# The RWKV-7 recurrence in two chains of four units instead of four chains of two, with its operands kept in DRAM records

## The chip, the cores and the metric

The kernel runs on one core of one Trainium2 chip. A core has engines that each work through a program of their own in order: TensorE (PE, matmuls; PEld are its weight loads), VectorE (DVE), ScalarE (ACT), GpSimd (POOL, which here only issues DMAs) and SyncE (SP, which issues the weight loads). They meet through semaphores. The metric is the device time of one execution in microseconds (us); lower is better.

## What is computed

One decoder layer on x of 256 tokens by 4096 columns, all in float32. Cut to what matters:

```python
h = rms_norm(x, norm_pre_g)
proj = einsum('btd,dc->btc', h, w_in)          # 4096 -> 14528 columns
rwkv_in, g_rwkv, glu_v, glu_g, g_conv = split(proj, ...)
xs = rwkv_in + (shift(rwkv_in) - rwkv_in) * mu_shift
r, k, v, w_low, a_low = split(xs, ...)
# 32 heads of 64; per step t and head, with a state S of 64 x 64:
S = S * w_t + (S @ -kk_t) b_t^T + v_t k_t^T ;  y_t = S @ r_t
y_rwkv = (group_norm(y) + bonus) * silu(g_rwkv)
c = silu(layer_norm(causal_conv31(glu_v * sigmoid(glu_g)))) @ w_pw2 + b_pw2
y_conv = c * silu(g_conv)
out = concat(y_rwkv, y_conv) @ w_out
return x + rms_norm(out, norm_post_g)
```

The recurrence is done in chunks of 32 tokens (8 chunks), with matrices inside a chunk and the state S handed from chunk to chunk.

## The kernel before

**The main stream.** The three projections (w_in, w_pw2, w_out) are 41 blocks of mostly 512 columns. A block runs through k-tiles of 128 rows, and one k-tile of a block is a slot: 1248 slots, each with six matmuls of 512 columns (two halves of the tokens, each with hi by hi, hi by lo and lo by hi, since a float32 product is made of fp32r parts). For each slot SP loads weights (`wr`, 512 KB for two slots, four buffers), ACT rounds them (`wh`), DVE takes the rest (`wl`), each with five buffers, three to four slots ahead of PE.

**The side work.** All that stands between the projections (the token shift, the preparation of the recurrence, its chain, the conv, the norms, the gates) is written as generators in lanes. After each slot's six matmuls `side.step()` lets the lanes go on; a generator that says `yield` gives up the rest of this slot, so that what follows it stands at least one slot later. The meters (`Meter`) add up an estimated cost on DVE and ACT and stop the lanes of a slot when these are ahead of PE. PE, DVE and ACT run in the order in which the code is written down; POOL and SP are ordered by a scheduler. Almost every instruction goes through the meter's line 92, so tiles and not lines tell them apart.

**The recurrence.** The 32 heads are 8 units of 4 heads. `job_prep(u)` makes a unit's operands: `c_ar` (decayed r and kk), `c_q` (masked products inside chunks, by PE), `c_bkt` (decayed b and k, turned by PE) and `c_uv` (v, turned). `job_inv(pr)` inverts the triangular parts of two units on DVE, by way of the DRAM tiles `n_dr` and `x_dr`, into `c_x`. `job_chain(pr)` takes a pair of units through the 8 chunks together. Per chunk PE has three visits to the PSUM tile `pz`, between them ACT and DVE:

- RY: `c_q` by `c_uv`, and from the second chunk on `c_ar` by the state `c_s`; then ACT copies the sum to `c_ry`;
- RU: `c_x` by `c_ry`; then ACT and DVE, half the rows each, write it negated into `c_uv`;
- RD and RO: `c_bkt` by `c_uv` (the state's change, not in the last chunk) and `c_q` by `c_uv` (the outputs); then DVE makes the outputs `c_y` and the next `c_s`.

Each of these products is 8 matmuls in the program for a pair (2 units by 4 quadrants of the array); the trace shows two records for each, so 16. A chain is 24 visits, the four pairs make 96. After a chain come a group norm over `c_y` and the store of the unit's result to `y_dr`. The conv's layer norm and the gates (`job_ln`, `job_gate`) wait in `open_conv` for the last chain, since they take over the SBUF of the recurrence; the w_pw2 blocks, from slot 928 on, need the layer norm's `chl`.

Of the kernel before, what the change touches and what calls it, by code (L numbers as in the profile page):

```python
# [9 lines left out]
F32 = mybir.dt.float32  # L10
F32R = mybir.dt.float32r
AF = mybir.ActivationFunctionType
# [5 lines left out]
P = 128  # L18
# [159 lines left out]
def hybrid(ctx: ExitStack, tc, a, out):  # L178
# [18 lines left out]
    sgc_dr = dr.tile([4, P, 1024], F32, name="sgc_dr")  # L197
    n_dr = dr.tile([8, 4, 8, CH, CH], F32, name="n_dr")
# [54 lines left out]
    def tp_put():  # L253

        tpf[0] += 1
# [29 lines left out]
    def x_load(i):  # L285
        if i % 2 == 0:
            st["xc"] = rw["pool"].tile([P, 8, T + 1], F32, name=XTAG[i // 2], bufs=1)
        t = st["xc"][:, 4 * (i % 2):4 * (i % 2) + 4, :]
# [138 lines left out]
    def job_prep(u):  # L427
# [71 lines left out]
        pr, un = u // 2, u % 2  # L499
        if un == 0:  # L500
            while pr and not rw.get(("chained", pr - 1)):
                yield "wait"
            rw["pair", pr] = dict(ar=rp.tile([P, 2, 16, 64], F32, name="c_ar", bufs=1),
                                  qs=rp.tile([P, 2, 2, NCH, 64], F32, name="c_q", bufs=1),
                                  bkt=rp.tile([P, 2, NCH, 2, 64], F32, name="c_bkt", bufs=1),
                                  uv=rp.tile([P, 2, NCH, 2, 64], F32, name="c_uv", bufs=1),
                                  pc=one.tile([P, 2, 16], F32, name="c_pc"))
        pair = rw["pair", pr]
        ar, qs, bkt, uv, pc = (pair[k][:, un] for k in ("ar", "qs", "bkt", "uv", "pc"))
# [46 lines left out]
        rw[("n", u)] = True  # L556

        bp = yield from head_sums(bq, "t_sw")
        if un == 0:
            while pr and not rw.get(("done", pr - 1)):  # L560
                yield "wait"
            pair["bv"] = rp.tile([P, 2, 512], F32, name="c_bv", bufs=1)
        vec.tensor_tensor(out=pair["bv"][:, un], in0=bp, in1=vs[:, 0:512], op=ALU.mult)
# [11 lines left out]
        for h in range(2):  # L575
            for e in range(2):
                act(out=uv[:, e::2, h], in_=t[h], func=AF.Copy)
            tp_put()
        rw[("prepd", u)] = True
        yield  # L580

    def job_inv(pr):

        rp = rw["pool"]
        while ("n", 2 * pr + 1) not in rw or (pr and not rw.get(("done", pr - 1))):
            yield "wait"
# [24 lines left out]
        xt = rp.tile([P, 2, 8, CH], F32, name="c_x", bufs=1)  # L611
# [7 lines left out]
        rw["pair", pr]["xt"] = xt  # L619

    def job_chain(pr):

        rp = rw["pool"]
        while ("prepd", 2 * pr + 1) not in rw or "xt" not in rw["pair", pr]:
            yield "wait"
        d = rw.pop(("pair", pr))
        ar, qs, bkt, uv, pc, bv, xt = (d[k] for k in ("ar", "qs", "bkt", "uv", "pc", "bv", "xt"))
        ys = rp.tile([P, 4, 2, 2, 64], F32, name="c_y", bufs=1)
        S = pz = ry = None
        RY, RU, RO, RD = (slice(i * 64, i * 64 + 64) for i in range(4))  # L630
        UN = range(2)
# [4 lines left out]
        def outputs(c):  # L636
            for rows in (slice(0, P),) if c % 2 == 0 else KS:
                vec.tensor_tensor(out=ys[rows, c // 2], in0=swap(pz[rows, :, :, RO]), in1=ry[rows], op=ALU.add)

        for c in range(NCH):  # L640
            vr, ur = VR[c % 2], UR[c % 2]
            if c > 0:
                outputs(c - 1)
                Sn = rp.tile([P, 2, 2, 64], F32, name="c_s", bufs=2)
                dec = pc[:, :, c - 1::8].unsqueeze(3).broadcast_to([P, 2, 2, 64])
                if S is None:
                    vec.tensor_tensor(out=Sn, in0=swap(pz[:, :, :, RD]), in1=dec, op=ALU.mult)
                else:
                    vec.tensor_tensor(out=Sn, in0=swap(pz[:, :, :, RD]), in1=S, op=ALU.add)
                    vec.tensor_tensor(out=Sn, in0=Sn, in1=dec, op=ALU.mult)  # L650
                S = Sn
                yield
            pz = ps_ch.tile([P, 2, 2, 256], F32, name="pz")

            for n in UN:
                for q, h in DIAG:
                    pe.matmul(pz[HS[q], h, n, RY], qs[vr[q ^ h], n, h, c, :], uv[vr[q ^ h], n, c, h, :], start=n == 0, stop=S is None and n == 1)
            for n in UN if S is not None else ():
                for q, h in DIAG:
                    pe.matmul(pz[HS[q], h, n, RY], ar[HS[h], n, q * 8 + c, :], S[HS[h], n, q, :], start=False, stop=n == 1)  # L660
            yield
            ry = rp.tile([P, 2, 2, 64], F32, name="c_ry", bufs=1)
            act(out=ry, in_=swap(pz[:, :, :, RY]), func=AF.Copy)
            for n in UN:
                for q, h in DIAG:
                    pe.matmul(pz[ur[q ^ h], h, n, RU], xt[ur[q], n, h * 4 + c // 2, :], ry[ur[q], n, h, :], start=True, stop=True)
            yield
            act(out=uv[ur[0], :, c], in_=swap(pz[ur[0], :, :, RU]), func=AF.Copy, scale=-1.0)
            vec.tensor_scalar(out=uv[ur[1], :, c], in0=swap(pz[ur[1], :, :, RU]), scalar1=-1.0, scalar2=None, op0=ALU.mult)
            for n in UN if c < NCH - 1 else ():  # L670
                for q, h in DIAG:
                    pe.matmul(pz[HS[h], q, n, RD], bkt[HS[q ^ h], n, c, h, :], uv[HS[q ^ h], n, c, h, :], start=True, stop=True)
            for n in UN:
                for q, h in DIAG:

                    ro, k0 = (KS, CH) if c % 2 else (HS, 0)
                    pe.matmul(pz[ro[q], h, n, RO], qs[ur[q ^ h], n, h, c, k0:], uv[ur[q ^ h], n, c, h, :], start=True, stop=True)
            yield
        outputs(NCH - 1)
        rw[("chained", pr)] = True  # L680
        yield 0

        mv = rp.tile([P, 2, 16], F32, name="c_mv", bufs=1)
        mn, vr = mv[:, 0], mv[:, 1]
        y3 = ys.rearrange("p c n h x -> p (c n h) x")
        for b in range(2):
# [4 lines left out]
        for b in range(2):  # L691
# [15 lines left out]
        for b in range(2):  # L707
# [5 lines left out]
        for n in UN:  # L713
            u = 2 * pr + n
            yo = rp.tile([P, 16, CH], F32, name="c_sq", bufs=1)
            bv3 = bv[:, n].rearrange("p (c t) -> p c t", t=CH)
# [12 lines left out]
            if n == 0:  # L729
                for _ in range(6):  # L730
                    yield
        rw[("done", pr)] = True
# [156 lines left out]
    def ev_shift(kind, g):  # L889
        def f(acc):  # L890
# [6 lines left out]
            if kind == "v":  # L897
# [3 lines left out]
                side.add("2", job_chain(g))  # L901
# [31 lines left out]
    def open_conv():  # L933
        while not rw.get(("done", 3)):
            yield "wait"
# [322 lines left out]
```

## Time and profile before

| | |
|---|---|
| median of 3 runs | 1850.20 us (1850.18 to 1852.35) |
| the profiled execution's own time | 1850.36 us |
| its span, first to last instruction | 1848.5 us |
| PE busy | 1835.3 us (99%) |
| DVE busy | 1345.9 us (73%) |
| ACT busy | 1024.4 us (55%) |
| POOL busy | 118.3 us (6%), 218 instructions |
| DMA | 367.19 MB, mean 199 GB/s |

PE's clock is granted in full (0.998 in the mean, that is 2.4 GHz). A busy PE here counts each matmul to its modelled end, which lies after the start of the next one; what a stretch of PE really costs is read from the starts in the timeline.

### The profile page before, as it was taken

What the parts mean: (1) busy time and instruction counts of PE and PEld (TensorE: products, weight loads), DVE (VectorE), ACT (ScalarE), POOL (GpSimd) and SP (SyncE); (2) the same over time, 40 slices, a digit from 0 to 9 for tenths busy, and PEclk for the clock granted to TensorE, in tenths of its full rate; (3) what the DMA queues carried; (4) which work ended last, traced back from release to release, by engine and by line L of the source; (5) the groups of instructions that cost most, each with busy time, mean ns of one, the idle gap of its engine ahead of it and who ended that gap; (6) DMA issues with size and microseconds to landing.
All of it is one profiled execution on the core that took longest, in us unless ns stands there. A gap on an engine that the chain in (4) does not pass through costs nothing.

```text
span 1848.5 us, 31244 instructions
## 1 busy us (share of the span) xinstructions
PE 1835.3 (99%) x11569; PEld 1495.3 (81%) x11569; DVE 1345.9 (73%) x2630; ACT 1024.4 (55%) x1785; POOL 118.3 (6%) x218
## 2 busy tenths in 40 slices
PE   9999999999999999999999999999999999999997
PEld 7899888877888877888778888788888888888886
DVE  6655679987689988799877899667656655555555
ACT  6756665546655555655465655356645444445453
POOL 0000001300000300011200003010000000000000
PEclk9999999999999999999999999999999999999999
DMA  9867667755667746676546677468776766666665
GB/s 329 271 177 203 177 180 198 215 148 146 191 189 204 205 124 180 179 206 197 163 143 200 175 223 217 147 208 277 214 233 204 246 194 199 199 200 194 204 198 190
DMA packets 193863, 367.19 MB, mean 199 GB/s; under 512 B 14384, under 2 KB 31920, under 8 KB 193456
## 3 DMA queue, kind: packets, MB, share of 16 engines
q1 hardware_dynamic: 182352, 335.31, 60.7%
q0 software_dynamic: 11360, 29.90, 5.3%
q8 instruction: 90, 1.47, 0.3%
q14 instruction: 61, 0.50, 0.1%
HBM read 352.57 MB, written 12.58 MB: 198 GB/s over the span
## 4 chain that ended last, share of the span: by engine, by line
PE 98%; DVE 1%; DMA 0%; ACT 0%; SPq 0%; issue 0%; DVEq 0%
PE acc L92 92%; PE tp L92 4%; PE pz L92 3%; DMA wr<-in_w_in 0%; DVE chl L92 0%; DVE wl L92 0%; DVE t_pi L92 0%; ACT L92 0%; SPq L291 0%; ACT wh L92 0%; DVE c_y L92 0%; SPq L1104 0%; ACT tp L92 0%; DVEq L1236 0%; ACT t_sw L92 0%
## 5 line engine op out<-in xcount | busy, mean ns | idle before, releaser
L92 ACT ACTIVATE wh<-wr 128x512 fp32r<-128x512 f32 (+1 forms) x1243 | 770.4, 624 | 655.2 <-PE acc L92 372.4
L92 DVE TENSOR_TENSOR wl<-wr,wh 128x512 fp32r<-128x512 f32 (+1 forms) x1243 | 831.5, 677 | 339.9 <-ACT wh L92 335.4
L92 PE MATMUL acc<-wh,lh 128*128 128x512 f32 (+1 forms) x2358 | 927.9, 394 | 1.0 <-ACT wh L92 0.9
L92 PE MATMUL acc<-wl,lh 128*128 128x512 f32 (+1 forms) x2358 | 911.0, 386 | 0.5 <-DVE wl L92 0.5
L92 PE MATMUL acc<-wh,ll 128*128 128x512 f32 (+1 forms) x2358 | 911.1, 386 | 0.0
L92 PEld LDWEIGHTS acc<-wh,lh 128*128 128x128 f32 x2358 | 442.8, 188 | 92.5 <-ACT wh L92 2.1
L92 PEld LDWEIGHTS acc<-wh,ll 128*128 128x128 f32 x2358 | 442.8, 188 | 89.3
L92 PEld LDWEIGHTS acc<-wl,lh 128*128 128x128 f32 x2358 | 443.2, 188 | 83.5 <-DVE wl L92 1.5
L92 DVE SCALAR_TENSOR_TENSOR cw<-up,pv,cw 128x256 f32<-128x256 f32 x480 | 216.6, 477 | 0.4
L92 PE MATMUL acc<-wh,chl 128*128 128x512 f32 x256 | 82.5, 397 | 0.0
L92 PEld LDWEIGHTS acc<-wh,chl 128*128 128x128 f32 x256 | 48.1, 188 | 11.1
L92 DVE TENSOR_SCALAR c_uv<-pz 32x256 f32<-32x256 f32 x32 | 13.6, 426 | 51.7 <-ACT c_uv L92 51.7
L92 PE MATMUL acc<-wl,chl 128*128 128x512 f32 x128 | 50.5, 395 | 0.0
L554 POOL DMA_DIRECT2D n_dr<-c_q x32 | 18.6, 589 | 489.0 <-DVE c_q L92 438.3
L92 ACT ACT_TABLE_LOAD x38 | 48.8, 1283 | 1.8 <-PEq L1230 0.7
L615 POOL DMA_DIRECT2D c_x<-x_dr x64 | 34.8, 551 | 14.0 <-DMA x_dr<-t_x 11.0
L92 ACT ACTIVATE c_ry<-pz 128x256 f32<-128x256 f32 x32 | 12.3, 384 | 41.0 <-PE pz L92 31.5
L92 ACT ACTIVATE pt<-acc,rstd 128x512 f32<-128x512 f32 (+3 forms) x52 | 34.0, 657 | 1.7 <-PE acc L92 1.0
L92 DVE TENSOR_TENSOR c_sq<-t_x,c_y 128x120 f32<-128x120 f32 (+24 forms) x124 | 31.8, 257 | 4.0 <-DMA c_y<-n_dr 3.9
L92 DVE TENSOR_TENSOR t_x<-t_x,c_sq 128x120 f32<-128x120 f32 (+24 forms) x124 | 31.7, 256 | 0.1
L92 PEld LDWEIGHTS pz<-c_uv,c_q 32*64 32x64 f32 (+1 forms) x1024 | 19.7, 124 | 14.3 <-issue 12.0
L92 DVE RECIPROCAL t<-t 128x128 f32<-128x128 f32 x32 | 29.8, 940 | 0.3
(172 smaller groups left out, 876.3 us busy)
## 6 DMA issues: line engine op xcount, KB each, us to landing
wr<-in_w_in SPq DMA_DIRECT2D x431, 512.0 KB, 4.2
wr<-in_w_out SPq DMA_DIRECT2D x128, 512.0 KB, 4.4
wr<-in_w_pw SPq DMA_DIRECT2D x32, 512.0 KB, 4.4
wr<-in_w_in SPq DMA_DIRECT2D x16, 352.0 KB, 3.3
c_y<-n_dr POOLq DMA_DIRECT2D x16, 256.0 KB, 6.3
out<-chl SPq DMA_DIRECT2D x16, 256.0 KB, 2.2
wr<-in_w_in SPq DMA_DIRECT2D x16, 192.0 KB, 2.7
wr<-in_w_in SPq DMA_DIRECT2D x16, 160.0 KB, 2.5
```

Of the source, the lines that this page charges most:

```text
L92: return f(*args, **kw)
L554: nc.gpsimd.dma_start(out=n_dr[u, y].rearrange("(h g) k j -> k h g j", h=2), in_=qs[y * CH:(y + 1) * CH, :, 1 - x::2, x * CH:(x + 1) * CH])
L615: nc.gpsimd.dma_start(out=xt[y * CH:(y + 1) * CH, un, h * 4:h * 4 + 4], in_=x_dr[2 * pr + un, y ^ (2 * h), h * 4:h * 4 + 4].rearrange("g i ...
```

## The change

The chains become two, each of four units (a quad) in lockstep, so every product of a visit has 16 matmuls in the program instead of 8. The operands no longer stay in SBUF from preparation to chain: `job_prep` writes `c_ar`, `c_q`, `c_bkt` and `c_uv` of its unit to the DRAM tile `rec_dr` (and the bonus to `bv_dr`), and the chain fetches a record of 1 MB per chunk into `c_st` (two buffers), one chunk ahead. The three tiles RY, RU and RO now lie in the same columns of `pz` (RX). A chunk has more `yield`s between its steps. The inversion of the second pair no longer waits for the first chain. The chain is started only by every second group of columns, and `open_conv` waits for the second quad. The x tiles of the start lie in other buffers.

```diff
@@ job_prep
-        pr, un = u // 2, u % 2
+        qd, un = u // 4, u % 4
         if un == 0:
-            while pr and not rw.get(("chained", pr - 1)):
-                yield "wait"
-            rw["pair", pr] = dict(ar=rp.tile([P, 2, 16, 64], F32, name="c_ar", bufs=1),
...
+            rw["quad", qd] = dict(pc=rp.tile([P, 4, 16], F32, name="c_pc", bufs=2))
+        pc = rw["quad", qd]["pc"][:, un]
+        ar = rp.tile([P, 16, 64], F32, name="c_ar", bufs=1)
+        qs = rp.tile([P, 2, NCH, 64], F32, name="c_q", bufs=1)
...
+        for h in range(2):
+            nc.gpsimd.dma_start(out=rec_dr[qd, :, :, un, 0, h * 64:h * 64 + 64].rearrange("c p x -> p c x"), in_=ar[:, h * 8:h * 8 + 8, :])
+            nc.gpsimd.dma_start(out=rec_dr[qd, :, :, un, 1, h * 64:h * 64 + 64].rearrange("c p x -> p c x"), in_=qs[:, h])
...
+        nc.gpsimd.dma_start(out=bv_dr[u], in_=bv)
...
+        for i, t in ((2, bkt), (3, uv)):
+            nc.gpsimd.dma_start(out=rec_dr[qd, :, :, un, i].rearrange("c p x -> p c x"), in_=t.rearrange("p c h x -> p c (h x)"))
@@ job_inv
-        while ("n", 2 * pr + 1) not in rw or (pr and not rw.get(("done", pr - 1))):
+        while ("n", 2 * pr + 1) not in rw or (pr > 1 and not rw.get(("done", pr // 2 - 1))):
@@ job_chain
+        UN = range(4)
+        def fetch(c):
+            if c < NCH:
+                recs[c] = rp.tile([P, 4, 4, 2, 64], F32, name="c_st", bufs=2)
+                nc.gpsimd.dma_start(out=recs[c].rearrange("p n i h x -> p (n i h x)"), in_=rec_dr[qd, c].rearrange("p n i x -> p (n i x)"))
...
+        fetch(0)
+        for _ in range(8):
+            yield
         for c in range(NCH):
+            fetch(c + 1)
+            ar, qs, bkt, uv = (recs[c][:, :, i] for i in range(4))
             if c > 0:
                 outputs(c - 1)
...
                 yield
+                yield
-            pz = ps_ch.tile([P, 2, 2, 256], F32, name="pz")
+            pz = ps_ch.tile([P, 2, 4, P], F32, name="pz")
...
             yield
-            ry = rp.tile([P, 2, 2, 64], F32, name="c_ry", bufs=1)
-            act(out=ry, in_=swap(pz[:, :, :, RY]), func=AF.Copy)
+            ry = rp.tile([P, 4, 2, 64], F32, name="t_x", bufs=1)
+            act(out=ry, in_=swap(pz[:, :, :, RX]), func=AF.Copy)
+            yield
...
-            act(out=uv[ur[0], :, c], in_=swap(pz[ur[0], :, :, RU]), func=AF.Copy, scale=-1.0)
-            vec.tensor_scalar(out=uv[ur[1], :, c], in0=swap(pz[ur[1], :, :, RU]), scalar1=-1.0, scalar2=None, op0=ALU.mult)
+            act(out=uv[ur[0]], in_=swap(pz[ur[0], :, :, RX]), func=AF.Copy, scale=-1.0)
+            vec.tensor_scalar(out=uv[ur[1]], in0=swap(pz[ur[1], :, :, RX]), scalar1=-1.0, scalar2=None, op0=ALU.mult)
+            yield
...
+            bv = rp.tile([P, 512], F32, name="t_x", bufs=1)
+            nc.gpsimd.dma_start(out=bv, in_=bv_dr[u])
+            for _ in range(6):
+                yield
@@ ev_shift, open_conv
-                side.add("2", job_chain(g))
+                if g % 2:
+                    side.add("2", job_chain(g // 2))
-        while not rw.get(("done", 3)):
+        while not rw.get(("done", 1)):
```

**PE at the start of a chain.** The order of PE's matmuls from the first RU visit to the RD and RO visit of chunk 0, in the first chain; `acc` rows are the main stream, six to a slot. Before:

```order
L92 MATMUL pz<-c_ry,c_x 32x64 x8
L92 MATMUL acc<-wh,lh 128x512
L92 MATMUL acc<-wl,lh 128x512
L92 MATMUL acc<-wh,ll 128x512
L92 MATMUL acc<-wh,lh 128x512
L92 MATMUL acc<-wl,lh 128x512
L92 MATMUL acc<-wh,ll 128x512
L92 MATMUL pz<-c_uv,c_bkt 64x64 x8
L92 MATMUL pz<-c_uv,c_q 64x64 x8
```

With the change the same two visits stand two slots apart, twelve main matmuls instead of six (left out here), and the second is one row of 32, since RD and RO read the same tile `c_st`:

```order
L92 MATMUL acc<-wh,lh 128x512
L92 MATMUL acc<-wl,lh 128x512
L92 MATMUL acc<-wh,ll 128x512
L92 MATMUL pz<-t_x,c_x 32x64 x16
L92 MATMUL acc<-wh,lh 128x512
L92 MATMUL acc<-wl,lh 128x512
L92 MATMUL acc<-wh,ll 128x512
```

What moved: each visit carries twice the matmuls, and it stands one slot further from the visit that it depends on. Over the whole program `pz` is visited 48 times instead of 96, with the same 1216 matmuls in all; the six matmuls of every slot stay as they were.

**POOL around the first chain.** The queue of DMA issues with the change, from the last inversion before the chain (`x_dr`, `c_x`) on; in the kernel before, the load of the next inversion's `t_x` and the conv's `c_dr` follow right behind `c_x` there:

```order
L647 DMA c_st<-rec_dr 128x2048 x2
L794 DMA c_dr<-cw 128x512
L615 DMA x_dr<-t_x 256x1x32 x8
L623 DMA c_x<-x_dr 32x4x32 x16
L647 DMA c_st<-rec_dr 128x2048
L794 DMA c_dr<-cw 128x512
L647 DMA c_st<-rec_dr 128x2048 x4
L560 DMA rec_dr<-c_ar 128x8x64 x2
L647 DMA c_st<-rec_dr 128x2048
L561 DMA rec_dr<-c_q 128x8x64
```

What moved: the eight fetches of a quad stand in the same queue as the record writes of the next unit and the conv's stores, and the first two go out before the inverse is stored. POOL has 282 rows in all instead of 202.

**DVE before the w_pw2 blocks.** The end of the layer norm on DVE, before; `wl` rows are the main stream's, one per slot, and the last `chl` row here stands behind 886 of them:

```order
L92 TENSOR_TENSOR chl<-c_c,chl 128x1024
L92 TENSOR_TENSOR wl<-wr,wh 128x512
L92 SCALAR_TENSOR_TENSOR c_m<-ln_q,pv,tp 128x256 x2
L92 TENSOR_TENSOR c_c<-c_c,ln_r 128x1024
L92 TENSOR_TENSOR wl<-wr,wh 128x512 x9
L92 TENSOR_TENSOR chl<-c_c,chl 128x1024
L92 TENSOR_TENSOR wl<-wr,wh 128x512 x21
```

With the change the last `chl` row stands behind 937 of them:

```order
L92 TENSOR_TENSOR chl<-c_c,chl 128x1024
L92 TENSOR_TENSOR wl<-wr,wh 128x512
L92 TENSOR_TENSOR c_c<-c_c,ln_r 128x1024
L92 TENSOR_TENSOR wl<-wr,wh 128x512 x8
L92 TENSOR_TENSOR chl<-c_c,chl 128x1024
L92 TENSOR_TENSOR wl<-wr,wh 128x512 x2
L92 SCALAR_TENSOR_TENSOR c_m<-ln_q,pv,tp 128x256 x2
```

What moved: the layer norm ends 51 slots later. PE reads its last quarter from slot 940 on.

## Rows read from the trace of the kernel before

**Rows 1.** The page: engines' busy time, and the chain that ended last.

```profile
PE 1835.3 (99%) x11569; PEld 1495.3 (81%) x11569; DVE 1345.9 (73%) x2630; ACT 1024.4 (55%) x1785; POOL 118.3 (6%) x218
...
PE acc L92 92%; PE tp L92 4%; PE pz L92 3%; DMA wr<-in_w_in 0%; DVE chl L92 0%; DVE wl L92 0%; DVE t_pi L92 0%; ACT L92 0%; SPq L291 0%; ACT wh L92 0%; DVE c_y L92 0%; SPq L1104 0%; ACT tp L92 0%; DVEq L1236 0%; ACT t_sw L92 0%
```

**Rows 2.** Waits of ACT: who for whom, us, times, longest us.

```profile
ACT wh L92 <- PE acc L92: 372.4, 532, 3.5
ACT wh L92 <- DMA wr<-in_w_in: 13.6, 9, 2.4
```

**Rows 3.** PE's timeline, RU to RO visit of chunk 0: start, us, what.

```profile
380.42 0.39 PE L92 MATMUL acc<-wh,ll 128*128 128x512 f32 x1
380.74 0.42 PE L92 MATMUL pz<-c_ry,c_x 32*32 32x64 f32 x16
...
381.43 0.39 PE L92 MATMUL acc<-wl,lh 128*128 128x512 f32 x1
381.66 0.39 PE L92 MATMUL acc<-wh,ll 128*128 128x512 f32 x1
...
382.36 0.40 PE L92 MATMUL acc<-wh,ll 128*128 128x512 f32 x1
382.68 0.46 PE L92 MATMUL pz<-c_uv,c_bkt 64*64 64x64 f32 x16
383.07 0.46 PE L92 MATMUL pz<-c_uv,c_q 32*64 32x64 f32 x16
...
383.80 0.40 PE L92 MATMUL acc<-wl,lh 128*128 128x512 f32 x1
```

**Rows 4.** PE's timeline, the first RY visit, which has one product only.

```profile
378.44 0.39 PE L92 MATMUL acc<-wh,ll 128*128 128x512 f32 x1
378.76 0.46 PE L92 MATMUL pz<-c_uv,c_q 32*64 32x64 f32 x16
...
379.49 0.40 PE L92 MATMUL acc<-wl,lh 128*128 128x512 f32 x1
```

**Rows 5.** PE's timeline, two longer visits of the same small shape, in the preparation.

```profile
217.42 0.39 PE L92 MATMUL acc<-wh,ll 128*128 128x512 f32 x1
217.74 1.16 PE L92 MATMUL tp<-c_ar,t_bk 64*64 64x64 f32 x64
...
219.17 0.39 PE L92 MATMUL acc<-wl,lh 128*128 128x512 f32 x1
...
231.39 0.39 PE L92 MATMUL acc<-wh,ll 128*128 128x512 f32 x1
231.71 0.69 PE L92 MATMUL tp<-cst,t_bk 64*64 64x64 f32 x32
...
232.67 0.39 PE L92 MATMUL acc<-wl,lh 128*128 128x512 f32 x1
```

**Rows 6.** The timeline of ACT and DVE between the visits of rows 3.

```profile
381.23 0.37 ACT L92 ACTIVATE c_uv<-pz 32x256 f32<-32x256 f32 x1 [1.03 <-PE pz L92]
...
381.64 0.43 DVE L92 TENSOR_SCALAR c_uv<-pz 32x256 f32<-32x256 f32 x1 [2.15 <-ACT c_uv L92]
```

**Rows 7.** Instructions of 512 columns by tile: ns min/median/max, first and last start.

```profile
L92 DVE TENSOR_TENSOR c_y<-c_y,c_mv x16: 680/688/693, 449.4 to 1225.3; 128x512 f32<-128x512 f32 x16
...
L92 ACT ACTIVATE c_sq<-c_y x8: 615/618/633, 450.2 to 1218.8; 128x512 f32<-128x512 f32 x8
```

**Rows 8.** DMA: POOL's queue (packets, MB, share), and one issue (KB, us to landing).

```profile
q0 software_dynamic: 11360, 29.90, 5.3%
...
c_c<-in_x POOLq DMA_DIRECT2D x1, 2048.0 KB, 11.1
```

**Rows 9.** Busy time and DMA of 1225 to 1300 us, where the layer norm's loads run.

```profile
1225.00:1300.00 75.00, 75.00 (x340) 62.04 (x339) 53.33 (x78) 45.12 (x70) 7.43 (x14) 1.00 0.81 260
```

**Rows 10.** Waits of ACT in that same stretch.

```profile
ACT wh L92 <- DMA wr<-in_w_in: 8.8, 5, 2.3
```

More of the change, by code (lines that the diff above doesn't have):

```diff
@@ L556, in job_prep @@
         rw[("n", u)] = True
+        for h in range(2):
+            nc.gpsimd.dma_start(out=rec_dr[qd, :, :, un, 0, h * 64:h * 64 + 64].rearrange("c p x -> p c x"), in_=ar[:, h * 8:h * 8 + 8, :])
+            nc.gpsimd.dma_start(out=rec_dr[qd, :, :, un, 1, h * 64:h * 64 + 64].rearrange("c p x -> p c x"), in_=qs[:, h])
         bp = yield from head_sums(bq, "t_sw")
[L559 to L563, printed above, removed]
+        bv = rp.tile([P, 512], F32, name="c_bv", bufs=1)
+        vec.tensor_tensor(out=bv, in0=bp, in1=vs[:, 0:512], op=ALU.mult)
+        nc.gpsimd.dma_start(out=bv_dr[u], in_=bv)
         tp_put()
@@ L610, in job_inv @@
                 nc.gpsimd.dma_start(out=xv[rho][:, un], in_=xi[rho * 32:(rho + 1) * 32, un])
-        xt = rp.tile([P, 2, 8, CH], F32, name="c_x", bufs=1)
+        quad = rw["quad", pr // 2]
+        if pr % 2 == 0:
+            quad["x"] = rp.tile([P, 4, 8, CH], F32, name="c_x", bufs=1)
+        xt = quad["x"][:, pr % 2 * 2:pr % 2 * 2 + 2]
         for y in range(4):
@@ L618, in job_inv, with job_chain @@
             yield
-        rw["pair", pr]["xt"] = xt
-    def job_chain(pr):
+        if pr % 2:
+            quad["xt"] = quad["x"]
+    def job_chain(qd):
         rp = rw["pool"]
-        while ("prepd", 2 * pr + 1) not in rw or "xt" not in rw["pair", pr]:
+        while ("prepd", 4 * qd + 3) not in rw or "xt" not in rw["quad", qd]:
             yield "wait"
-        d = rw.pop(("pair", pr))
-        ar, qs, bkt, uv, pc, bv, xt = (d[k] for k in ("ar", "qs", "bkt", "uv", "pc", "bv", "xt"))
-        ys = rp.tile([P, 4, 2, 2, 64], F32, name="c_y", bufs=1)
+        d = rw.pop(("quad", qd))
+        pc, xt = d["pc"], d["xt"]
+        ys = rp.tile([P, 4, 4, 2, 64], F32, name="c_y", bufs=1)
         S = pz = ry = None
-        RY, RU, RO, RD = (slice(i * 64, i * 64 + 64) for i in range(4))
-        UN = range(2)
+        RX, RD = slice(0, 64), slice(64, 128)
+        UN = range(4)
+        recs = {}
+        def fetch(c):
+            if c < NCH:
+                recs[c] = rp.tile([P, 4, 4, 2, 64], F32, name="c_st", bufs=2)
+                nc.gpsimd.dma_start(out=recs[c].rearrange("p n i h x -> p (n i h x)"), in_=rec_dr[qd, c].rearrange("p n i x -> p (n i x)"))
         def swap(x):
@@ L676, in job_chain @@
                     ro, k0 = (KS, CH) if c % 2 else (HS, 0)
-                    pe.matmul(pz[ro[q], h, n, RO], qs[ur[q ^ h], n, h, c, k0:], uv[ur[q ^ h], n, c, h, :], start=True, stop=True)
+                    pe.matmul(pz[ro[q], h, n, RX], qs[ur[q ^ h], n, h, k0:], uv[ur[q ^ h], n, h, :], start=True, stop=True)
             yield
         outputs(NCH - 1)
-        rw[("chained", pr)] = True
         yield 0
-        mv = rp.tile([P, 2, 16], F32, name="c_mv", bufs=1)
+        mv = rp.tile([P, 2, 32], F32, name="c_mv", bufs=1)
         mn, vr = mv[:, 0], mv[:, 1]
         y3 = ys.rearrange("p c n h x -> p (c n h) x")
-        for b in range(2):
+        for b in range(4):
             sl = slice(b * 8, b * 8 + 8)
@@ L690, in job_chain @@
         vec.tensor_scalar(out=mn, in0=mn, scalar1=1.0 / 64, scalar2=None, op0=ALU.mult)
-        for b in range(2):
+        for b in range(4):
             sl = slice(b * 8, b * 8 + 8)
@@ L706, in job_chain @@
         vec.reciprocal(out=vr, in_=vr)
-        for b in range(2):
+        for b in range(4):
             sl = slice(b * 8, b * 8 + 8)
@@ L728, in job_chain @@
             nc.gpsimd.dma_start(out=y_dr[u], in_=yo.rearrange("p c t -> p (c t)"))
[L729 to L732, printed above, removed]
+        rw[("done", qd)] = True
         yield
```

37 lines of the change are left out of this document (19 added, 18 removed).

## The prediction

> **What bounds the kernel now.** I read four views, in this order. First the page's busy times and the chain that ended last: PE is busy 99% of the span, and 92% of the chain is main matmuls (`acc`), 4% transposes and 3% the recurrence's `pz` [rows 1]. So an edit is worth what it takes from PE's own stream of instructions, and nothing else counts unless it becomes later than PE. Second the waits: ACT stood 372.4 us idle until PE gave it a buffer back, but only 13.6 us, in 9 pieces, for weights to land [rows 2]. Both feeders run ahead and are held back by PE, so there is room on ACT and DVE and in the weight stream. Third PE's timeline around the visits to `pz`, for what a visit costs. Busy time can't tell that, since it overlaps; I take starts. Two main matmuls that follow each other start 0.23 us apart (381.43 to 381.66, [rows 3]). A visit's cost is the time from the start of the last main matmul ahead of it to the start of the second one behind it, less two such gaps (0.46 us), because the first matmul behind a visit is slow too. Fourth the DMA rows, for what the records add.
>
> **What the change removes: half of the visits.** A visit with two products of 16 records (RD and RO, or RY with the state) costs 383.80 - 382.36 - 0.46 = 0.98 us. A visit with one product of `c_x` costs 381.43 - 380.42 - 0.46 = 0.55 us [rows 3]. A visit with one product of `c_q` costs 379.49 - 378.44 - 0.46 = 0.59 us [rows 4]. A pair's chain has 14 visits of the first kind (7 RY and 7 RD with RO), 8 RU, and 2 with one product (the first RY, the last RO): 14 x 0.98 + 8 x 0.55 + 2 x 0.59 = 19.3 us. Four pairs: 77.2 us.
>
> **What stays: the matmuls, in longer groups.** Their number is the same, so the question is what a product of 32 records costs beside one of 16. The trace of before has no such `pz` visit, but it has longer visits of the same 64x64 shape over the same four quadrants: 64 records cost 219.17 - 217.42 - 0.46 = 1.29 us, and 32 cost 232.67 - 231.39 - 0.46 = 0.82 us [rows 5]. Thirty-two more records cost 0.47 us, so sixteen more cost 0.235 us. The rest of a visit is paid once per product, however long. That gives 0.98 + 2 x 0.235 = 1.45 us for a double visit, 0.55 + 0.235 = 0.785 for RU and 0.59 + 0.235 = 0.825 for a single one. A quad's chain: 14 x 1.45 + 8 x 0.785 + 2 x 0.825 = 28.2 us; two quads 56.5 us. **The gain on PE is 77.2 - 56.5 = 20.7 us.** The other end of this cost: from the start of the first product to that of the second in a double visit are 383.07 - 382.68 = 0.39 us [rows 3]; if sixteen more records cost all of that again, visits come to 1.76, 0.94 and 0.98 us, a quad to 14 x 1.76 + 8 x 0.94 + 2 x 0.98 = 34.1 us, and the gain is 77.2 - 68.2 = 9.0 us. Below that, at no gain, a product would have to cost twice as much when doubled, and rows 5 exclude it. More than 20.7 us would need the added records to be nearly free, which rows 5 exclude as well. I take 20.7 us, by the nearer rows: same shape, same quadrants, same length as the new groups.
>
> The Trainium skill has a rule that speaks for the lower end: "TensorE: Matmul & The Clock Gate", in the section "Wait — 56ns, not 53.3ns?", says that matmuls never start closer together than about 25 ns, however small they are. By it sixteen more records would cost some 0.40 us. The trace bears it out only in the look of one product (0.39 us for 16); the 64 records that take 1.16 us in all [rows 5], 18 ns each, speak against it, and they count for more.
>
> **What it adds between the visits.** DVE and ACT do the same steps on twice the columns in half as many instructions, so they are relieved. What matters is whether a step is ready when PE comes to the next visit. The tightest hand-over now is RU to RO: the visit starts at 380.74, ACT copies from 381.23 for 0.37 us, DVE from 381.64 for 0.43 us [rows 6], that is to 382.07, and PE comes at 382.68 [rows 3], 0.61 us later. At 512 columns ACT takes 0.62 and DVE 0.69 us [rows 7], 0.51 us more together; the longer RU visit moves both sides by the same 0.235 us, and from its end to RO stand two slots instead of one, 6 x 0.23 = 1.38 us more. The slack grows to 0.61 - 0.51 + 1.38 = 1.5 us. From RO to the next RY DVE has at most four steps of 0.69 us (two outputs, two for the state), 2.8 us, in three or four slots, 4.1 to 5.5 us. So the wider steps cost PE nothing; the cover is the slack just worked out.
>
> **What it adds in DMA.** Per unit 6 record writes and a bonus, 8 x 7 = 56 issues; 16 fetches and 8 loads of the bonus: 80 more on POOL, 0.54 us of POOL each by 118.3 us for 218 instructions [rows 1], 43 us on an engine that is 6% busy. The bytes are 16 MB of records written, 16 read and 4 of bonus. POOL's queue has 29.90 MB at 5.3% of the DMA engines' time [rows 8], so 37.7 (in the page's MB) add about 6.7%. A fetch is one more wait for PE: RY needs the record. The fetch of chunk c+1 can go once RO of chunk c-1 has released the buffer, and RY of c+1 stands 11 slots behind that in the order: 11 x 1.38 us and three visits (1.45 + 0.785 + 1.45), 18.9 us. A load of twice its size landed in 11.1 us [rows 8]. Queued ahead of a fetch on POOL are at most the conv's store and the next unit's record writes, which wait for values that DVE has made some slots earlier. That cover is large, so I cost the fetch at nothing.
>
> **What it moves.** The second quad's chain ends later, and with it the layer norm, by 51 slots. Its last quarter stands behind 937 `wl` rows and is needed at slot 940. DVE is held to PE's pace by five `wl` buffers, so it comes to that row when PE is near slot 933: about 7 x 1.38 = 9.7 us early, where it was some 58 slots early before. No visit and no wait of PE is added there. From slot 943 on the program is the same as before.
>
> **Sum.** The profiled execution took 1850.36 us (span 1848.5 and 1.9 us around it), 0.16 us from the median of 1850.20. 1850.2 - 20.7 = **1829.5 us**, 1.1% less.
>
> **The rivals.**
>
> *Longer groups cost more than rows 5 say.* Gain 9.0 us, **1841.2 us**. For it: `pz` products change their operands per unit and were seen only at 16 records, 0.39 us each. Against it: 64 records in rows 5. The rule on the 25 ns, named above, would end here too, at 0.40 us for each sixteen and about 1841.5 us.
>
> *The layer norm comes late.* Its loads of 2 MB now run with the gates close behind, in 60 slots less room; in the stretch of its loads ACT waited 8.8 us for weights, up to 2.3 us at a time [rows 10], while DMA was at 0.81 and PE lost nothing [rows 9]. If that, and a chain of DVE and ACT steps that slips, outruns the 9.7 us by as much as those 8.8 us, PE waits 8.8 us: **1838.3 us**.
>
> *The hand-overs give it back: no change.* It takes 20.7 / 48 = 0.43 us of waiting per visit. The slack of 1.5 us at the tightest place speaks against it; for it speaks that DVE's queue has conv and preparation between the steps, and is full where the fifth unit is prepared beside the first chain. **About 1850 us.**
>
> *Slower: the fetches starve the weights.* Sixteen fetches of 1 MB come in bursts beside a stream whose weights are needed every two slots. The place is `wh` on ACT in the chain. The largest burst of before, in rows 9 and 10, cost ACT up to 2.3 us at a time, and PE rode over it on the four slots that ACT is ahead, about 5.5 us. If every fetch cost PE those 2.3 us in full, 16 x 2.3 = 36.8 us, the time is 1829.5 + 36.8 = **1866.3 us**. It decides from 20.7 / 16 = 1.3 us per fetch on. Against it: the stock of slots and the 13.6 us in the whole kernel [rows 2]. The Trainium skill, "DMA: Bandwidth & Descriptors", section "Queues, rings and completion order", states the mechanism: an engine takes turns between its queues by packets, so that a second queue takes its share from the weights at once. No row here shows one packet waiting for another; what it would do is what rows 10 show.
>
> *That the change doesn't do what it says* is excluded by the order: 48 visits, and 16 matmuls in each product.
>
> **How the numbers follow.** Forecast 0.67 (own range 1825 to 1834: rounding of starts by 0.01 us over 96 visits, and the 2 us by which the runs differ), longer groups 0.11, late layer norm 0.07, no change 0.07, slower 0.08. A difference of 0.2%, 3.7 us, is about what a measurement of this kernel can tell from none. Faster: 0.67 + 0.11 + 0.07 = 0.85; same 0.07; slower 0.08. The range takes in the first three, 1825 to 1844.
>
> **What would show it.** In the profile of the changed kernel a double visit should take 1.45 us by starts, RU 0.785, with no idle of PE ahead of `pz`; POOL's queue about 68 MB and 12%; PE's idle no more than before; ACT's waits for weights a few tens of us at most. A visit of 1.76 us would show the first rival, PE idle ahead of `acc` with `chl` as the releaser the second, ahead of `pz` the third, and PE idle for `wh` inside the two chains the last. I am wrong at the root if PE's starts show the visits halved and the time the same, for then PE was not what set the pace.

## The result and the profile after

The changed kernel takes 1829.6 us (median of four runs, 1828.7 to 1830.2) beside 1851.1 us of the kernel before on the same chip: a ratio of 0.988, 95% interval 0.987 to 0.990, faster by 21.5 us. The profiled execution took 1830.16 us, 20.2 us less than that of before.

The page of the changed kernel, with the lines that answer to [rows 1] and [rows 8]; columns are the same:

```profile
span 1828.1 us, 31382 instructions
...
PE 1814.0 (99%) x11569; PEld 1492.9 (82%) x11569; DVE 1330.3 (73%) x2560; ACT 1009.2 (55%) x1745; POOL 179.4 (10%) x298
...
q0 software_dynamic: 19808, 67.65, 11.7%
...
PE 93%; DMA 2%; DVE 2%; issue 2%; POOL 1%; ACT 0%; SPq 0%; DVEq 0%; POOLq 0%; ACTq 0%
```

PE has the same 11569 instructions, is busy 21.3 us less and still fills 99% of the span. POOL's queue moves 67.65 MB. In the chain that ended last PE's share has fallen from 98 to 93%; DMA, DVE and time without a visible cause ("issue") have 2% each, POOL 1%. Where they stand is shown below.

Three visits to `pz`, in PE's timeline of the changed kernel (start, us, what): the first RY, RY with the state, and RU. They answer to [rows 3, 4].

```profile
620.26 0.39 PE L92 MATMUL acc<-wh,ll 128*128 128x512 f32 x1
620.58 0.69 PE L92 MATMUL pz<-c_st 32*64 32x64 f32 x32
...
621.54 0.40 PE L92 MATMUL acc<-wl,lh 128*128 128x512 f32 x1
...
1127.91 0.39 PE L92 MATMUL acc<-wh,ll 128*128 128x512 f32 x1
1128.23 0.69 PE L92 MATMUL pz<-c_st 32*64 32x64 f32 x32
1128.85 0.69 PE L92 MATMUL pz<-c_s,c_st 64*64 64x64 f32 x32
1129.48 0.50 PE L92 MATMUL acc<-wh,lh 128*128 128x512 f32 x1
1129.81 0.39 PE L92 MATMUL acc<-wl,lh 128*128 128x512 f32 x1
...
1132.10 0.39 PE L92 MATMUL acc<-wh,ll 128*128 128x512 f32 x1
1132.42 0.65 PE L92 MATMUL pz<-t_x,c_x 32*32 32x64 f32 x32
...
1133.34 0.39 PE L92 MATMUL acc<-wl,lh 128*128 128x512 f32 x1
```

By the prediction's way of counting (start to start, less 0.46 us) the single visit costs 621.54 - 620.26 - 0.46 = 0.82 us, the double one 1129.81 - 1127.91 - 0.46 = 1.44 us and RU 1133.34 - 1132.10 - 0.46 = 0.78 us. PE never waited in front of a `pz` product. The tightest hand-over, RU to RD, is this one in the first chain's chunk 0 (DVE's half of the copy, then PE's visit):

```profile
625.49 0.70 DVE L92 TENSOR_SCALAR c_st<-pz 32x512 f32<-32x512 f32 x1 [2.30 <-ACT c_st L92]
...
627.69 1.32 PE L92 MATMUL pz<-c_st 64*64 64x64 f32 x64
```

DVE ends at 626.19 us, 1.50 us ahead of PE; the least in the 16 chunks is 1.34 us.

The waits of PE in the changed kernel (who for whom, us in total, times, longest), and ACT's waits for PE and for weights, beside [rows 2]:

```profile
PE acc L92 <- ACT wh L92: 1.4, 3, 0.8
PE acc L92 <- DVE wl L92: 1.3, 5, 0.5
PE tp L1184 <- DVE eps L92: 1.2, 1, 1.2
...
ACT wh L92 <- PE acc L92: 382.5, 559, 3.3
ACT wh L92 <- DMA wr<-in_w_in: 35.3, 19, 5.9
```

PE's waits behind `wh`, `wl` and `pz` were 1.8 us in all before; now they are 2.7 us. ACT's waits for weights have grown from 13.6 us in 9 pieces to 35.3 us in 19, the longest from 2.4 to 5.9 us. Of PE's 2.7 us 1.6 lie in the first 12 us; behind that PE waits three times.

The first of the three comes 4 us ahead of the first quad's fetches, which go out at 531.15 us (timelines of DVE and PE):

```profile
525.67 0.22 DVE L92 TENSOR_TENSOR c_sq<-t_x,c_y 128x62 f32<-128x62 f32 x1 [3.47 <-DMA c_y<-n_dr]
...
526.94 0.50 PE L92 MATMUL acc<-wl,lh 128*128 128x512 f32 x1 [0.46 <-DVE wl L92]
```

DVE stood 3.47 us for the inversion's load of `c_y` from `n_dr`, and the `wl` behind it in DVE's order came late. This load runs beside the last record writes; such loads take 8.5 us in the median, 6.3 us in the kernel before. The other two waits are at the second quad. The chain of the changed kernel shows both places (start, us, what), and PE's timeline behind it the two waits:

```profile
515.64 9.91 DMA c_y<-n_dr
...
1018.67 9.34 DMA c_y<-n_dr
...
1035.86 9.69 DMA wr<-in_w_in
...
1047.06 34.10 PE acc L92 x149
```

```profile
1046.33 0.50 PE L92 MATMUL acc<-wh,lh 128*128 128x512 f32 x1 [0.46 <-ACT wh L92]
1047.06 0.50 PE L92 MATMUL acc<-wl,lh 128*128 128x512 f32 x1 [0.22 <-DVE wl L92]
```

A weight load that takes 4.4 us in the median took 9.7 us, and PE stood 0.46 and 0.22 us. Around it POOL's queue holds the last record writes of the preparation, the first two fetches of the second quad, which go out together, and the store of a gate, `sgc_dr` (512 KB; POOL's timeline):

```profile
1025.25 0.89 POOL L583 DMA_DIRECT2D rec_dr<-c_uv  x1 [2.78 <-ACT c_uv L92]
1033.62 1.11 POOL L647 DMA_DIRECT2D c_st<-rec_dr  x2 [7.49 <-issue]
1038.46 0.54 POOL L954 DMA_DIRECT2D sgc_dr<-pt  x1 [3.72 <-ACT pt L92]
```

By the landings in the packed trace the last record write was there at 1033.07 us, so the fetches follow the writes and don't overlap them; they landed at 1039.8 and 1043.7 us, the gate's store at 1045.7 us, the weight load at 1045.6 us. The DMA engines moved 389 GB/s from 1035 to 1040 us, beside 222 GB/s in the mean. The quad's first visit comes at 1115.6 us, so these two megabytes are sent for some 80 us early. In the chain the weight load stands behind an inversion's load of 9.3 us too, and behind the DVE work that had waited for it (1028.0 to 1035.8 us).

### The profile page after: what moved, and what is told of

Its sections match the earlier page's. It is cut to its first block, busy times and chain, and to the rows that moved or that the text cites. A ratio compares the mean times of both kernels' runs of the same rounds, so it can differ in the third digit from the quotient of the medians.

```text
span 1828.1 us, 31382 instructions
## 1 busy us (share of the span) xinstructions
PE 1814.0 (99%) x11569; PEld 1492.9 (82%) x11569; DVE 1330.3 (73%) x2560; ACT 1009.2 (55%) x1745; POOL 179.4 (10%) x298
## 3 DMA queue, kind: packets, MB, share of 16 engines
q0 software_dynamic: 19808, 67.65, 11.7%
## 4 chain that ended last, share of the span: by engine, by line
PE 93%; DMA 2%; DVE 2%; issue 2%; POOL 1%; ACT 0%; SPq 0%; DVEq 0%; POOLq 0%; ACTq 0%
PE acc L92 87%; PE tp L92 3%; PE pz L92 3%; DMA c_y<-n_dr 1%; DMA wr<-in_w_in 1%; DVE wl L92 1%; DMA n_dr<-c_q 0%; DVE t L92 0%; DVE chl L92 0%; POOL n_dr L556 0%; POOL c_y L598 0%; POOL rec_dr L560 0%; ACT wh L92 0%; ACT L92 0%; DVE cw L92 0%
## 5 line engine op out<-in xcount | busy, mean ns | idle before, releaser
L560 POOL DMA_DIRECT2D rec_dr<-c_ar x16 | 14.4, 902 | 328.4 <-DVE c_ar L92 327.8
L92 PEld LDWEIGHTS pz<-c_st 32*64 32x64 f32 (+2 forms) x1472 | 25.0, 128 | 12.2 <-PE acc L92 4.9
L1027 POOL DMA_DIRECT2D bb<-in_norm_post_g x8 | 4.3, 539 | 303.3 <-DVE chl L92 258.8
L92 DVE TENSOR_SCALAR c_st<-pz 32x512 f32<-32x512 f32 x16 | 11.1, 693 | 31.1 <-ACT c_st L92 31.1
L92 PE MATMUL pz<-c_st 32*64 32x64 f32 (+2 forms) x1472 | 30.6, 222 | 0.0
```

Of the source, the lines that this page charges most:

```text
L92: return f(*args, **kw)
L560: nc.gpsimd.dma_start(out=rec_dr[qd, :, :, un, 0, h * 64:h * 64 + 64].rearrange("c p x -> p c x"), in_=ar[:, h * 8:h * 8 + 8, :])
L1027: nc.gpsimd.dma_start(out=gb, in_=a["norm_post_g"][0:1, j * BN:(j + 1) * BN].broadcast_to([P, BN]))
```

## The experiments

Each run stands beside runs of the kernel before on the same chip, 1850.1 to 1850.3 us in the median; ratios are to those.

**Lockstep or records?** The first kernel keeps the records, the fetches and the wider spacing, but takes the units in pairs again.

```diff
-        qd, un = u // 4, u % 4
+        qd, un = u // 2, u % 2
...
-        UN = range(4)
+        UN = range(2)
...
-                if g % 2:
-                    side.add("2", job_chain(g // 2))
+                side.add("2", job_chain(g))
```

> The records, the fetches and the wider spacing of the changed kernel stay, but four chains take two units each, so the 96 visits with products of 16 come back. If the gain is that PE pays fewer starts of products (my theory), this loses all of it: the changed kernel's 1829.6 us plus 20.7 us of visits, 1850 us, and 1 to 2 us more if the records cost anything. If the gain came from something else in the change (shorter queues on DVE and ACT, operands out of SBUF, more slots between steps), the time stays near 1830 us.

Measured: 1850.9 us (1849.9 to 1852.0), ratio 1.0005 (0.9995 to 1.0014). A double visit costs 0.95 to 0.98 us again and RU 0.55. The whole gain is the lockstep; going through DRAM gives nothing by itself, and costs here no more than the interval's upper end, 2.6 us.

**Do visits count, or products?** The second keeps the 48 visits, and splits each double visit into four products of 16.

```diff
-            for n in UN:
-                for q, h in DIAG:
...
-            for n in UN if S is not None else ():
-                for q, h in DIAG:
...
+            for m in ((0, 1), (2, 3)):
+                for n in m:
+                    for q, h in DIAG:
...
+                for n in m if S is not None else ():
+                    for q, h in DIAG:
```

> Quads and 48 visits as in the changed kernel, but inside a double visit the two products alternate between the first and the second two units, so that there are four products of 16 records instead of two of 32. If each product has a start of its own to pay (theory: a second product of 16 adds 0.98 - 0.59 = 0.39 us to a visit, 0.235 of it for its matmuls, so 0.155 us for its start), the 28 double visits take 2 x 0.155 us more each, 8.7 us: 1838.3 us, and a double visit 1.75 us. If only the number of visits counts, it stays at 1829.6 us and 1.44 us.

Measured: 1837.6 us (1836.0 to 1839.7), ratio 0.9933 (0.9918 to 0.9947). PE's timeline of this kernel, an RY visit:

```profile
647.98 0.39 PE L92 MATMUL acc<-wh,ll 128*128 128x512 f32 x1
648.30 0.46 PE L92 MATMUL pz<-c_st 32*64 32x64 f32 x16
648.69 0.46 PE L92 MATMUL pz<-c_s,c_st 64*64 64x64 f32 x16
649.08 0.46 PE L92 MATMUL pz<-c_st 32*64 32x64 f32 x16
649.47 0.46 PE L92 MATMUL pz<-c_s,c_st 64*64 64x64 f32 x16
...
650.20 0.40 PE L92 MATMUL acc<-wl,lh 128*128 128x512 f32 x1
```

The visit costs 650.20 - 647.98 - 0.46 = 1.76 us. Products of 16 start 0.39 us apart, products of 32 in the changed kernel 0.62 us (1128.23 to 1128.85): sixteen more records cost 0.23 us, and each product that is opened another 0.16 us. That is why a longer product is cheaper than two, and the 28 split visits account for 28 x 0.32 = 9.0 us by the rows, 8 us by the medians. The change opens 76 products instead of 152; at this price that is 76 x 0.16 = 12 us of its 21 us, an estimate, and the rest goes to the 48 visits that are gone.

One thing is not varied by this edit: each product that it opens also has another shape on the array than the one before it (rows by columns, 32*64 and 64*64). The same kernel has a visit in which a product of the preparation, with the same 64*64, follows the last one:

```profile
727.49 0.46 PE L92 MATMUL pz<-c_st 32*64 32x64 f32 x16
727.88 0.46 PE L92 MATMUL pz<-c_s,c_st 64*64 64x64 f32 x16
728.16 1.11 PE L92 MATMUL tp<-cst,t_bk 64*64 64x64 f32 x64
```

Where the shape changes, the next product starts 0.39 us later (727.49 to 727.88); where it stays, 0.28 us (727.88 to 728.16). The changed kernel has 0.62 and 0.51 us for products of 32 (724.08 to 724.71 to 725.22). These traces have four places without a change of shape, and all give 0.28 us for 16 and 0.51 us for 32. So 0.11 of the 0.16 us go with the change of shape, and some 0.05 us with the product itself.

**Were the added slots needed?** The third takes out the three slots that the change adds between a chunk's products.

```diff
                 S = Sn
                 yield
-                yield
...
-            yield
             for n in UN:
...
-            yield
             for n in UN if c < NCH - 1 else ():
```

> The three added places where a chunk gives up its slot are taken out, so the visits stand one slot apart again and RO to the next RY two or three. By the working of the prediction the slack from RU to RO is then 0.61 - 0.51 = 0.1 us and from RO to RY about 0.3 us in even chunks: PE waits little, 0 to 0.3 us at some of 48 places, 1830 to 1835 us. If the added slots are what makes the change pay (rival), PE waits at every visit, and some 0.4 us at 48 places give the whole gain back, 1850 us.

Measured: 1828.7 us (1827.3 to 1830.7), ratio 0.9887 (0.9871 to 0.9904). That is below the 1830 to 1835 us expected. One `pz` product waited, 0.18 us for DVE's half of the copy into `c_st`. The prediction put the slack at the tightest hand-over at 1.5 us, of which the slot is 1.38 us. What is left without it, 0.1 us, is what the chip shows: in most chunks DVE ends its half 0.11 to 0.14 us ahead of PE, so PE need not wait.

**What do the transfers cost?** The fourth fetches every record twice.

```diff
+                for _ in range(2):
-                nc.gpsimd.dma_start(out=recs[c]...
+                    nc.gpsimd.dma_start(out=recs[c]...
```

> Every record is fetched twice, one after the other, into the same buffer: 16 MB more, and a fetch is there after about 2 x 6.1 + 1 = 13 us. If 18.9 us are to be had between the release of the buffer and the visit that needs it (theory), and the weights live with the bursts, the time stays within 1.5 us of 1829.6. If a fetch costs PE something by taking DMA time from the weights (the slower rival at 2.3 us per fetch), 16 more cost up to 36.8 us, 1866 us; half of that shows too.

Measured: 1834.8 us (1833.6 to 1837.2), ratio 0.9919 (0.9904 to 0.9933). This missed: 5 us more, not 1.5 us at most. Laid beside the changed kernel product by product, the profile loses 5.1 us between 1023 and 1081 us and 0.7 us between 1304 and 1325 us. It differs by up to 0.9 us either way ahead of the first chain and by 0.3 us between the chains, and by 0.01 us inside the two chains, where 12 of the 16 extra transfers run. PE's timeline at the place:

```profile
1046.05 0.49 PE L92 MATMUL acc<-wh,lh 128*128 128x512 f32 x1 [0.62 <-ACT wh L92]
...
1049.20 0.40 PE L92 MATMUL acc<-wh,ll 128*128 128x512 f32 x1
1051.94 0.67 PE L92 MATMUL acc<-wh,lh 128*128 128x512 f32 x1 [2.35 <-ACT wh L92]
...
1053.69 0.63 PE L92 MATMUL acc<-wh,lh 128*128 128x512 f32 x1
1054.12 0.63 PE L92 MATMUL acc<-wl,lh 128*128 128x512 f32 x1
```

The weight load behind it took 13.2 us. So I formed a second theory: the price is not in the amount but at this one place, where the first two fetches of a quad follow right behind the last record writes. The next kernels test it, by extra fetches and by moving one.

**Extra fetches away from the place, and many of them.** One fetches only the records of chunks 2 to 7 twice; another fetches every record four times, which asks how far the cover inside a chain reaches.

```diff
+                for _ in range(2 if c > 1 else 1):
```

> Records of chunks 2 to 7 are fetched twice, those of chunks 0 and 1 once: three quarters of the doubled kernel's extra transfers (12.6 of 16.8 MB) remain, and what is gone is the second 2 MB at each start of a chain. If the doubled kernel's 5.2 us came from the place (the first two fetches of a chain go out together, right behind the last record writes, and the weight loads beside them land late), this is back at 1829.6 to 1830.5 us and the wait of 2.35 us in front of a main product near 1050 us is gone. If it came from the amount of the transfers, three quarters of it stay: about 1833.5 us.

Measured: 1832.2 us (1830.5 to 1834.3), ratio 0.9903 (0.9889 to 0.9918). This lies between the two expectations. Its profiled execution again lost nothing inside the chains, and 2.23 us in one wait at 1046.8 us, behind a weight load of 12.1 us, although at that place it asks for the same transfers as the changed kernel. By itself this decides nothing.

```diff
+                for _ in range(4):
```

> Every record is fetched four times into the same tile, one transfer after the other. This asks how far the cover of a fetch reaches inside the chain. The window between two chunks was put at 18.9 us, and one fetch lands in 6.1 us (median of the changed kernel); four make 4 x 6.1 = 24.4 us, so that the first product of a chunk should wait about 5.5 us for its record, in the 6 chunks of each of the 2 sets of four whose fetch starts inside the chain: 12 x 5.5 = 66 us, and beside it about three times the 5.1 us that the doubled fetches cost at 1023 to 1085 us, 15 us: about 1910 us. The waits should stand in front of the first small product of chunks 2 to 7, put down to the DMA of the record. Rival: the fetches of one record run beside each other on the rings and land in less than 18.9 us together; then only the 15 us are lost and the time is near 1845 us.

Measured: 1925.6 us (1922.7 to 1927.7), ratio 1.0407 (1.0391 to 1.0422). PE's waits:

```profile
PE pz L92 <- DMA c_st<-rec_dr: 64.1, 7, 15.5
PE acc L92 <- ACT wh L92: 7.4, 9, 2.4
```

The total of the waits in front of `pz` is as expected (66 us), though in 7 long pieces and not 12 of 5.5 us. So the prediction's window of 18.9 us holds in size: two fetches fit, four don't. The time is 15 us above the expectation; PE's busy time grew by 20.6 us at an unchanged count, which the last section takes up.

**One fetch moved.** The fetch of chunk 1 is held until the inverse's matrices are there, by a copy of one element into its tile.

```diff
+                if c == 1:
+                    vec.tensor_copy(out=recs[c][0:1, 0, 0, 0, 0:1], in_=xt[0:1, 0, 0, 0:1])
                 nc.gpsimd.dma_start(out=recs[c]...
```

> The fetch of chunk 1 of each set of four is held until the inverse's matrices have arrived (a copy of one element into the record's tile ahead of the fetch), so that it no longer goes out right behind the fetch of chunk 0. By the same theory the weight load near 1036 us lands in less than 9.7 us, the two waits of 0.46 and 0.22 us in front of main products at 1046 and 1047 us go, and the time falls by up to 1 us, to about 1829 us, which is within what the comparison can tell; the rows have to show it. Rival: the weight load is late because of the record writes and the first fetch alone; then the two waits stay. If the copy or the later fetch stands in somebody's way, a wait of the first small product of chunk 1 appears and the time is above 1830 us.

Measured: 1827.1 us (1826.8 to 1827.6), ratio 0.9876 (0.9860 to 0.9893). POOL's timeline has one fetch at the place, and the other 78 us later:

```profile
1031.86 0.56 POOL L649 DMA_DIRECT2D c_st<-rec_dr  x1 [7.67 <-issue]
...
1109.99 0.56 POOL L649 DMA_DIRECT2D c_st<-rec_dr  x1 [13.59 <-DVE c_st L92]
```

Between 20 us and the end no main product waits: all of PE's 1.1 us behind `wh` and `wl` is in the first 20 us. ACT's waits for these weights fell from 35.3 to 19.9 us. The time fell by 2.5 us in the median where up to 1 us was expected. Laid beside it product by product, the changed kernel's profile loses 3.4 us: 0.7 in the first 20 us, 0.9 around the wait at 527 us, which lies ahead of the fetches, 0.3 at 820 to 840 us, and 1.5 between 1000 and 1070 us. Only the last is at the place, and it is about twice the 0.68 us of waits seen there.

**The two edits crossed.** Three kernels on one chip: the changed kernel once more; chunks 2 to 7 fetched twice with chunk 1's fetch held; and the held fetch together with the slots taken out.

> The changed kernel itself, unaltered, on the same chip and beside the next two, so that they can be set against it directly: about 1829.6 us, with the spread of 1828.7 to 1830.2 us that its four runs had, or a little wider if the late weight load near 1036 us lands differently from run to run.

> Records of chunks 2 to 7 fetched twice (12.6 MB more), with the fetch of chunk 1 held until the inverse's matrices are there. The kernel that doubled them without holding chunk 1 took 1832.2 us (1830.5 to 1834.3). If what it lost, and what it varied by, stands at the one place behind the last record writes, this is at 1827 to 1828 us, as the kernel that only holds chunk 1, with a spread of 1 us. If the amount of transfers costs by itself, it is at about 1830 us, the 1827.1 us of that kernel and 3 us more.

> Both edits that looked free or better together: the fetch of chunk 1 held, and the three added slots between a chunk's products taken out. No main product should wait between 20 and 1800 us, as in the kernel that only holds chunk 1, and one small wait of about 0.2 us may stand in front of a small product where the slots are tight: 1826.5 to 1827.5 us, 2 to 3 us below the changed kernel beside it. Rival: the spread of the kernel without the slots (1827.3 to 1830.7 us) came from its chains and not from the weight load; then it stays near 1828.7 us.

Measured: 1830.5 us (1829.1 to 1832.5) for the changed kernel, ratio 0.9890 (0.9873 to 0.9906); 1827.7 us (1827.4 to 1830.0), ratio 0.9879 (0.9864 to 0.9894), for the doubled fetches with the held one; 1828.8 us (1827.9 to 1829.6), ratio 0.9882 (0.9867 to 0.9897), for both edits. With 12 fetches more, but one out of the way, the kernel is 2.8 us below the changed one in the median, and their runs overlap at the edge. The profiles tell more, since they can be compared at the place alone. Between 1000 and 1070 us, beside the kernel that only holds the fetch, the changed kernel loses 1.5 and 1.9 us in its two profiles, the one with later fetches doubled 3.1 us, and the one with these doubled and the fetch held 0.3 us. That is the amount against the place, and the place decides. How much the changed kernel loses there changes from run to run: its profile here has a weight load of 11.3 us at 1035.4 us and a wait of 1.05 us behind it.

Two fetches that go out together are not enough for the loss. The kernel without the added slots sends both out at 1027.2 and 1027.7 us, and its profile loses nothing there. They have landed by 1036.4 us, before the gate's store goes out at 1038.2 us, whereas in the changed kernel the store goes out 5.2 us before the second fetch is there. That speaks for the store as a part of it, but doesn't show it: holding the store in place of the fetch was not tried.

Taking the slots out as well gives nothing more: 1828.8 us lies 1.3 us above the expectation's upper end, though no main product waits behind 20 us there and one small product waits 0.17 us. In the profiled execution (1829.6 us) 2.0 us over the kernel that only holds the fetch lie in the first 20 us, which neither edit touches, and 0.8 us in the first chain, as without the slots alone; for the other executions no trace shows it. Those first 20 us differ by up to 2.9 us between the profiles of these kernels, which is more than the held fetch gives. The lowest median is that of the kernel that only holds the fetch; it was not run on one chip with the changed kernel, and by the ratios to the kernel before the intervals of the two overlap.

**How early is the layer norm?** The convolution's normalization starts 16 slots later.

```diff
         if "pool" not in cv:
-            for _ in range(5):
+            for _ in range(21):
```

> The convolution's normalization starts 16 slots (about 18 us) later than in the changed kernel; nothing else is moved. By the prediction the pieces of its result were 9.7 us ahead of the products that read them, so that about 8 us of wait should stand in front of the blocks of the second convolution product, named as the wait for the normalized rows (chl) or their split: about 1838 us. Rival: the slots that follow give room enough, the work is only pushed into later slots that had nothing else to do, and the time stays at 1829.6 us.

Measured: 1841.6 us (1839.3 to 1843.3), ratio 0.9953 (0.9938 to 0.9968). PE's waits:

```profile
PE acc L92 <- ACT chl L92: 4.9, 2, 3.8
PE acc L92 <- DVE chl L92: 2.5, 2, 1.6
```

7.4 us of wait, named as expected; the time grew by 12 us (11 by the profiled executions), more than the waits. The expectation's 18 us for 16 slots is too low: at 1.38 us a slot they are 22 us, which less the 11 to 12 us lost leaves 10 to 11 us of margin. The changed kernel shows the margin itself (the last `chl` row on DVE, and the first product of PE that reads it):

```profile
1382.80 1.22 DVE L92 TENSOR_TENSOR chl<-c_c,chl 128x1024 fp32r<-128x1024 f32 x1
...
1393.75 0.62 PE L92 MATMUL acc<-wh,chl 128*128 128x512 f32 x2
```

The row ends at 1384.02 us, 9.7 us ahead of its reader.

## Why the prediction was right, and what it missed

- **PE sets the pace, so the gain is what leaves PE's stream.** Right. 21.3 us of busy time went and 20.2 us of the profiled execution. That the median came within 0.2 us of the 1829.5 us forecast is in part luck: the visits gave a little more than the 20.7 us, the new waits took it back, and the first 20 us of two profiles of the same changed kernel differ by 2.0 us.
- **Sixteen more records cost 0.235 us.** Right, and the step on which the time hung: double visits 1.44 us (1.45 predicted), RU 0.78 (0.785), single 0.82 (0.825). The 48 visits sum to 28 x 1.44 + 16 x 0.78 + 4 x 0.82 = 56.1 us, a gain of 21.1 us. With 0.9 us of new waits in front of PE this leaves 20.2 us. The rival of 0.39 us for each sixteen is shown to be something else by the second experiment: it holds 0.23 us for the records and 0.16 us for another product, most of that for its other shape. In the packed trace the records of a product start in fours, 7 ns apart within a four and 58 ns from one four to the next. The Trainium skill's 25 ns for every start ("TensorE: Matmul & The Clock Gate", section "Wait — 56ns, not 53.3ns?") would have put the double visit at about 1.78 us, as an estimate; the 1.44 us measured and the 7 ns speak against it here. By 0.40 us for each sixteen the prediction's sum comes to 1842.0 us and not to its 1841.5.
- **Wider steps on DVE and ACT are covered by 1.5 us.** Right: the slack measured is 1.50 us, and with the slot taken out PE waited 0.18 us once.
- **A fetch costs nothing, since it has 18.9 us inside the chain.** Right inside the chain, for one fetch and for two. It missed the chain's start: the first two fetches aren't bound to that window, go out as soon as the records are written, and run beside the weight stream together with a gate's store. The rival of starved weights was the right mechanism at the wrong place (the chains) and at a price too high (2.3 us for each of 16 fetches); it cost 1.5 and 1.9 us at the second quad's start in the changed kernel's two profiles, 0.7 and 1.3 us of it as waits of PE. The record writes, too, were put at nothing; the wait of 0.46 us at 527 us, which one of the two profiles has, stands beside them with no fetch out yet, behind an inversion's load of 9.9 us. By the Trainium skill ("DMA: Bandwidth & Descriptors", section "Queues, rings and completion order") a DMA engine takes turns, packet by packet, between the queues that have work for it. The weight load that lands in 9.7 us beside 2 MB of fetches and the store, and the waits that go when one of the two fetches is held, agree with that, though no row shows one packet waiting for another.
- **POOL.** The 80 issues were put at 43 us and took 61 us, because a record write (128 x 8 pieces of 64 or 128 numbers) takes 0.90 us there, not 0.54. POOL is idle enough that it made no difference.
- **The layer norm is 9.7 us early.** Right: 9.7 us in the changed kernel's trace.

## What to carry to other kernels

A short matmul group put between long ones costs a price per visit, a price per product, higher where the array's shape changes, and a price per record; batch so that products get longer, not only visits fewer, and read these prices from visits of other lengths that the trace already has. A prefetch that is free in the steady state can cost at its start, where nothing holds it back: look at when the first ones go out, what else is on the queues then, and how long before their use, and hold them with a dependency if they are early. Extra copies of a transfer are a good probe for this, if the two profiles are then compared place by place and not by their ends: here the first 20 us alone differed by more than what was looked for.

## What the hardware showed beyond what was expected

A wait in front of PE can cost more than its length. In the kernel with doubled fetches the granted clock was 1.00 in the stretches up to 1052 us; PE had stood 0.62 us at 1046 and then 2.35 us up to 1051.9, and the next stretches read (columns: window, busy us and count of each engine, granted clock, DMA share, GB/s):

```profile
1049.00:1052.00 3.00, 0.66 (x4) 0.22 (x2) 0.08 (x1) 0.74 (x2) 0.00 (x0) 1.00 0.99 401
1052.00:1054.00 2.00, 1.94 (x4) 1.27 (x5) 2.00 (x6) 1.46 (x3) 0.00 (x0) 0.53 1.05 393
1054.00:1056.00 2.00, 2.00 (x7) 1.52 (x7) 2.00 (x7) 1.36 (x3) 0.00 (x0) 0.62 0.71 163
1056.00:1060.00 4.00, 4.00 (x19) 3.32 (x18) 4.00 (x12) 1.73 (x3) 0.00 (x0) 1.00 0.69 231
```

The clock was near its lower level (1.2 of 2.4 GHz) for 3.5 us, and main products started 0.43 us apart, not 0.23. The late layer norm shows the same behind its waits of 1.65 and 3.79 us (granted clock 0.65 in 1391 to 1394 us and 0.57 in 1402 to 1406 us), and the kernel with four fetches 0.50 behind its first wait of 10.3 us; its 20.6 us of added busy time at an unchanged count fit that. A single wait of 2.23 us, in the kernel that doubled the later fetches, was followed by 1.00, and so was one of 2.36 us at 1094 us in the kernel with four fetches. What tells these apart wasn't tried.
